# Side work queued behind the newest split of weights on ScalarE and VectorE, and a first exponential on constants, in a Griffin-style decoder layer

## The chip, the core and the metric

One core of a Trainium2 chip runs the whole kernel. The metric is device time in microseconds, the median of the timed runs. Times inside the kernel come from one profiled execution; "at 73.25" is 73.25 us after that span's start. The engines are TensorE (PE; its weight loads are PEld), VectorE (DVE), ScalarE (ACT), GpSimd (POOL) and SyncE (SP, which here only issues DMAs). PSUM is the memory in which PE accumulates; SBUF is the working memory of all engines.

## What is computed

The reference is one decoder layer on 256 tokens of width 2048, in float32. Cut to what matters here:

```python
h = rmsnorm(x, norm_mix_g)
u = h @ w_in                                   # 2048 x 12288
c, b, xa, za, q, f, iv, og, ga, gb = split(u)  # 8 fields of 1024, 2 of 2048
ya = b * causal_dwconv3(c * xa, conv_w) * silu(za)
log_f = log(lb + (1 - lb) * sigmoid(f)); kk = (1 - lb) * sigmoid(-f)
o  = hgrn2_chunked(silu(q), kk, iv, log_f)     # gated linear recurrence, 8 heads of 128
yb = rmsnorm_per_head(o) * hg_norm_g * silu(og)
m  = sigmoid(ga) * (ya @ w_a_out) + sigmoid(gb) * (yb @ w_b_out)
x  = x + m @ w_o
x  = x + sigmoid(rmsnorm(x, ple_norm_g) @ w_ple_gate) * (p @ w_ple_proj)
return rmsnorm(x, final_norm_g)
```

## The kernel before

**Products in three parts.** A float32 product is made from two rounded halves of each factor: hi*hi + hi*lo + lo*hi. `split(pos)` makes the halves of a piece of weights of 256 x 512: ACT rounds `raw` to `whi` (L118), DVE subtracts to get `wlo` (L119). `put` does the same for activations (L152, L153, tiles `xh` and `xl`, and the like). `product` issues the three matmuls (L825, L826, L827), 128 x 128 by 128 x 512 each.

**Steps.** The list `steps` runs over all weights in pieces; a step has 12 matmuls (2 blocks of 128 rows of weights, 2 tiles of 128 tokens, 3 parts) and adds to the two PSUM banks of its group. A group is 512 columns of one product. In order: 16 groups of 8 steps for f, q, iv, og, c, xa, za, b, each field in two halves (f is steps 0 to 7, q 8 to 15, iv 16 to 23, og 24 to 31 and so on, to step 127); four rounds of ga, gb, A and B (8, 8, 4 and 4 steps, to step 223); four groups O (224 to 255); then PP (1 step) and PG (8 steps) four times: PP0 is 256, PG0 257 to 264, PG2 275 to 282, PP3 283 and the last PG 284 to 291. The last PG is written out by itself at the end, in three passes over its eight steps: all 512 columns for the first token tile in one bank, and two times 256 columns for the second.

**What comes ahead of PE.** `load` brings raw weights in pairs of steps, 1024 KB, in three buffers, on SP's DMA queue. `whi` and `wlo` have four buffers each, so split p of that pool can't start before step p-4 has ended; from step 286 on they come from a pool `late` with six buffers. Before the matmuls of step `pos`, the program makes splits up to `pos + ahead(pos)`; `ahead` is 3, and from step 277 on it grows by one a step to 8.

**Side work.** What follows a group's sums is written as generators, the epilogues `ep_f`, `ep_q` and so on: each copies its sums out of PSUM, computes, turns the result through DRAM (`turned`: four DMAs out, one back, then a transpose on DVE) and makes operands for later products. `advance()` lets every live epilogue go on to its next `yield` at the end of each step. Some that matter below: `ep_iv` copies the sums of iv into `v` (L202); `ep_f` takes logarithms (L264 to L268); `hgrn` starts with `y` (L377), makes exponentials and tiles `X` for products on PE (L324, L433, and L444 to L446, which read the tile `a` written at L328); `ep_pg` empties a PG group's two banks with a sigmoid on ACT (L615), and `ep_pp` a PP group's (L605). PSUM has four banks with the tag "g", two for each group, so a group takes the banks of the group two before it.

**Who sets the order.** The program text is not the order of the queues. A scheduler orders each engine's instructions when the kernel is compiled: it takes what it reckons to be ready, so side work may stand ahead of a split that comes earlier in the text, or far ahead of its own place. Buffers are handed out in the same pass. When the kernel runs, each engine takes its own queue in that fixed order. `tc.keep_in_program_order(ins)` puts one instruction behind everything traced before it on its engine. `tc.issue_after(ins)` is a block: what is traced in it on the engine of `ins` is queued behind `ins`; it adds no semaphore and touches no other engine.

## Time and profile before

| | |
|---|---|
| timed runs, median (lowest to highest of 3) | 838.65 us (838.03 to 839.04) |
| the profiled execution | 840.08 us |
| its span, first to last instruction | 838.3 us |
| mean granted PE clock | 0.994 |
| PE, PEld, DVE, ACT, POOL busy, us | 823.8, 683.5, 531.7, 432.7, 84.1 |
| DMA, mean over the span | 218 GB/s |

The profile gives, for groups of instructions, the line, the engine, the tiles written and read, the shapes and the count; then the busy time and the mean of one, and the idle time of the engine just before, with what ended it. A name such as whi stands for all buffers of that tile. In a timeline, each row has the start, the time taken and, in brackets, the idle time before it with its releaser. Matmuls overlap, and each row shows 0.39 us for one that follows the one before it after 0.23; a few matmuls are missing from the record, and rows of equal kind are merged (x2). The granted clock is the share of PE's full clock that was let through.

### The profile page before, as it was taken

What the parts mean: (1) busy time and instruction counts of PE and PEld (TensorE: products, weight loads), DVE (VectorE), ACT (ScalarE), POOL (GpSimd) and SP (SyncE); (2) the same over time, 40 slices, a digit from 0 to 9 for tenths busy, and PEclk for the clock granted to TensorE, in tenths of its full rate; (3) what the DMA queues carried; (4) which work ended last, traced back from release to release, by engine and by line L of the source; (5) the groups of instructions that cost most, each with busy time, mean ns of one, the idle gap of its engine ahead of it and who ended that gap; (6) DMA issues with size and microseconds to landing.
All of it is one profiled execution on the core that took longest, in us unless ns stands there. A gap on an engine that the chain in (4) does not pass through costs nothing.

```text
span 838.3 us, 9794 instructions
## 1 busy us (share of the span) xinstructions
PE 823.8 (98%) x3752; PEld 683.5 (82%) x3752; DVE 531.7 (63%) x600; ACT 432.7 (52%) x562; POOL 84.1 (10%) x76
## 2 busy tenths in 40 slices
PE   8998999999999999999999999999999999999995
PEld 5886888888888888888888888888888888888885
DVE  6557596794776686785655555545545665566672
ACT  7565564445564663545543543543443555565553
POOL 1001062001000152100001001001001000002110
PEclk9999999999999999999999999999999999999998
DMA  9975555646866555657657655655754878775442
GB/s 334 370 252 203 187 192 180 221 156 228 283 206 239 194 179 184 211 181 230 229 194 232 219 197 189 229 195 187 258 200 164 296 281 301 251 244 209 174 151 101
DMA packets 39792, 183.01 MB, mean 218 GB/s; under 512 B 4544, under 2 KB 13760, under 8 KB 21824
## 3 DMA queue, kind: packets, MB, share of 16 engines
q1 hardware_dynamic: 39312, 181.81, 62.6%
q8 instruction: 29, 0.48, 0.2%
q10 hardware_dynamic: 432, 0.56, 0.2%
q14 instruction: 19, 0.16, 0.1%
HBM read 170.82 MB, written 11.53 MB: 218 GB/s over the span
## 4 chain that ended last, share of the span: by engine, by line
PE 88%; issue 1%; ACT 0%; DVE 0%; POOLq 0%; POOL 0%
PE g L826 29%; PE g L827 29%; PE g L825 29%; PE s L324 1%; PE s L433 0%; PE s L445 0%; PE s L446 0%; PE s L444 0%; ACT xs L656 0%; DVE wlo L119 0%; ACT t L639 0%; DVE t L635 0%; POOLq L989 0%; POOL r L651 0%; ACT t L634 0%
## 5 line engine op out<-in xcount | busy, mean ns | idle before, releaser
L119 DVE TENSOR_TENSOR wlo<-raw,whi 128x1024 fp32r<-128x1024 f32 (+1 forms) x294 | 367.4, 1256 | 256.5 <-ACT whi L118 255.5
L118 ACT ACTIVATE whi<-raw 128x1024 fp32r<-128x1024 f32 (+1 forms) x294 | 308.0, 1053 | 338.1 <-PE g L827 313.0
L825 PE MATMUL g<-whi,xh 128*128 128x512 f32 (+1 forms) x912 | 353.2, 388 | 3.3 <-ACT whi L118 3.3
L826 PE MATMUL g<-wlo,xh 128*128 128x512 f32 (+1 forms) x912 | 352.7, 387 | 0.8 <-DVE wlo L119 0.8
L827 PE MATMUL g<-whi,xl 128*128 128x512 f32 (+1 forms) x912 | 351.9, 386 | 0.0
L825 PEld LDWEIGHTS g<-whi,xh 128*128 128x128 f32 x912 | 171.6, 188 | 38.9 <-ACT whi L118 5.1
L826 PEld LDWEIGHTS g<-wlo,xh 128*128 128x128 f32 x912 | 171.8, 188 | 36.1 <-DVE wlo L119 2.3
L827 PEld LDWEIGHTS g<-whi,xl 128*128 128x128 f32 x912 | 171.7, 188 | 34.3
L826 PE MATMUL g<-wlo,mh 128*128 128x512 f32 x128 | 49.6, 389 | 0.0
L825 PE MATMUL g<-whi,mh 128*128 128x512 f32 x128 | 49.5, 389 | 0.0
L827 PE MATMUL g<-whi,ml 128*128 128x512 f32 x128 | 49.5, 389 | 0.0
L569 POOL TENSOR_TENSOR t<-ga,gb 128x512 f32<-128x512 f32 x8 | 14.1, 1788 | 254.1 <-DVE gb L565 254.1
L827 PEld LDWEIGHTS g<-whi,ml 128*128 128x128 f32 x128 | 24.0, 188 | 5.0
L825 PEld LDWEIGHTS g<-whi,mh 128*128 128x128 f32 x128 | 24.0, 188 | 5.0
L826 PEld LDWEIGHTS g<-wlo,mh 128*128 128x128 f32 x128 | 24.0, 188 | 4.9
L825 PE MATMUL g<-whi,yaTh 128*128 128x512 f32 x64 | 24.9, 389 | 0.0
L826 PE MATMUL g<-wlo,yaTh 128*128 128x512 f32 x64 | 24.9, 389 | 0.0
L827 PE MATMUL g<-whi,yaTl 128*128 128x512 f32 x64 | 24.9, 389 | 0.0
L825 PE MATMUL g<-whi,ybTh 128*128 128x512 f32 x64 | 24.9, 389 | 0.0
L826 PE MATMUL g<-wlo,ybTh 128*128 128x512 f32 x64 | 24.9, 389 | 0.0
L827 PE MATMUL g<-whi,ybTl 128*128 128x512 f32 x64 | 24.9, 389 | 0.0
L352 POOL TENSOR_TENSOR X<-t,kT 128x256 f32<-128x256 f32 x12 | 11.1, 922 | 107.0 <-ACT t L366 71.7
(147 smaller groups left out, 542.1 us busy)
## 6 DMA issues: line engine op xcount, KB each, us to landing
raw<-in_w_in SPq DMA_DIRECT2D x91, 1024.0 KB, 4.8
raw<-in_w_o SPq DMA_DIRECT2D x16, 1024.0 KB, 5.8
raw<-in_w_pg SPq DMA_DIRECT2D x16, 1024.0 KB, 4.8
turn<-t SPq DMA_DIRECT2D x72, 128.0 KB, 2.7
t<-turn SPq DMA_DIRECT2D x18, 512.0 KB, 5.0
raw<-in_w_a SPq DMA_DIRECT2D x8, 1024.0 KB, 5.0
raw<-in_w_b SPq DMA_DIRECT2D x8, 1024.0 KB, 5.0
raw<-in_w_in SPq DMA_DIRECT2D x9, 512.0 KB, 7.7
```

What stands on the lines that cost most here:

```text
L118: nc.scalar.activation(out=hi[:, s], in_=src[:, s], func=AF.Copy)
L119: nc.vector.tensor_tensor(out=lo[:, s], in0=src[:, s], in1=hi[:, s].bitcast(F32), op=ALU.subtract)
L324: nc.tensor.matmul(bk[:, s], X[:, 0, h, :], X[:, 1, h, :], start=True, stop=True)
L352: eng.tensor_tensor(out=xv[:, w, :, :, half, :], in0=ev[:, :, blk, :, half, :], in1=src[:, :, blk, :, half, :], op=ALU.mult,)
L569: nc.gpsimd.tensor_tensor(out=spread(m, t), in0=blocks(ga[:, s]), in1=blocks(gb[:, s]), op=ALU.add)
L825: nc.tensor.matmul(psum, oh, hi, start=first, stop=False)
L826: nc.tensor.matmul(psum, oh, lo, start=False, stop=False)
L827: nc.tensor.matmul(psum, ol, hi, start=False, stop=last)
```

## The change

- `split` keeps its two newest instructions, one on ACT and one on DVE, in `state["splits"]`.
- A new function `step(e)` lets an epilogue run to its next `yield` inside `issue_after` of both. All calls of `next` on epilogues now go through it, those of `advance` and the first one of each epilogue. So what an epilogue puts on ACT or DVE is queued behind the newest split that the program had traced by then. In the steady part that is the split three steps ahead, later up to eight. POOL, PE and SP are not tied, and neither are `put_x`, `begin`, `add_squares`, `norm_of_x`, `last_half` and the last `last_norm`, which are not called through an epilogue.
- After the memset of the constant `mhalf`, an exponential of it is written to a new small tile `table`, the first ACTIVATE of the program.
- The pad at the head of the pool `small` grows from 8 to 64 columns, with its memset.

```diff
-PAD_CONST, PAD_SMALL = 8, 8
+PAD_CONST, PAD_SMALL = 8, 64
...
-        nc.scalar.activation(out=hi[:, s], in_=src[:, s], func=AF.Copy)
-        nc.vector.tensor_tensor(
+        a = nc.scalar.activation(out=hi[:, s], in_=src[:, s], func=AF.Copy)
+        v = nc.vector.tensor_tensor(
             out=lo[:, s], in0=src[:, s], in1=hi[:, s].bitcast(F32), op=ALU.subtract
         )
+        state["splits"] = (a.ins, v.ins)
...
     nc.gpsimd.memset(mhalf, -0.5)
+
+    nc.scalar.activation(out=sc(8, "table", 1), in_=mhalf, func=AF.Exp)
...
-    def advance():
-        for e in list(active):
+    def step(e):
+
+        a, v = state["splits"]
+        with tc.issue_after(a), tc.issue_after(v):
             try:
                 next(e)
             except StopIteration:
                 active.remove(e)
+
+    def advance():
+        for e in list(active):
+            step(e)
...
             active.append(ep_f(0, waiting))
-            next(active[-1])
+            step(active[-1])
...
             active.append(epilogues[kind](j, psum))
-            try:
-                next(active[-1])
-            except StopIteration:
-                active.pop()
+            step(active[-1])
```

## The prediction

> Steps are TensorE's, numbered 0 to 291 as in the section on the kernel; "split p" makes the high and low weights of step p.

> **What bounds the kernel now.** I read the page first: engine shares, clock, chain.

> ```profile
> PE 823.8 (98%) x3752; PEld 683.5 (82%) x3752; DVE 531.7 (63%) x600; ACT 432.7 (52%) x562; POOL 84.1 (10%) x76
> ...
> PEclk9999999999999999999999999999999999999998
> ...
> PE 88%; issue 1%; ACT 0%; DVE 0%; POOLq 0%; POOL 0%
> ```

> TensorE (PE) is busy for 98% of the span, and the chain that ended last is matmuls. VectorE (DVE) and ScalarE (ACT) matter only where they make PE wait. So the second view is the list of PE's waits (total us, times, longest):

> ```profile
> PE g L825 <- ACT whi L118: 3.3, 3, 1.7
> PE s L718 <- DVE warm L714: 1.5, 1, 1.5
> PE g L826 <- DVE wlo L119: 0.8, 2, 0.5
> ```

> That is little. Two of the waits for whi (1.35 and 0.26) and one of those for wlo lie in the first 11 us; the 1.72 and 0.53 left are one place, at 75 us. Third view, ACT's timeline there:

> ```profile
> 62.70 1.99 ACT L118 ACTIVATE whi<-raw 128x1024 fp32r<-128x1024 f32 x2
> ...
> 67.05 0.20 ACT L268 ACTIVATE lfl<-t 128x8 f32<-128x8 f32 x1
> 72.77 1.37 ACT L202 ACTIVATE v<-g,r1r 128x512 f32<-128x512 f32 x2 [5.52 <-PE g L827]
> 74.03 3.89 ACT L118 ACTIVATE whi<-raw 128x1024 fp32r<-128x1024 f32 x4
> ```

> ACT sits idle for 5.52 us until PE has finished step 23, because v, which reads that step's sums, stands ahead of splits 24 to 27. Split 24 is what PE needs next. Its weights were issued at 56.86 and landed 7.6 us later, at 64.4; those of 26 and 27 landed at 69.3. So order alone made PE wait. Fourth view, stretches there (busy us of PE, PEld, DVE, ACT, POOL, then the granted clock):

> ```profile
> 70.60:74.00 3.40, 2.81 (x13) 1.99 (x11) 2.21 (x2) 1.23 (x2) 1.17 (x2) 1.00 0.08 31
> 74.00:77.40 3.40, 1.74 (x6) 1.16 (x7) 2.29 (x2) 3.40 (x5) 0.00 (x0) 1.00 0.00 0
> 77.40:80.80 3.40, 3.40 (x9) 2.64 (x8) 3.40 (x4) 1.12 (x2) 0.00 (x0) 0.51 0.36 82
> ```

> After a stretch in which PE was idle for 49% (1.66 of 3.40), the clock is granted at half for 3.4 us.

> **The gain at 75 us.** A split of step p takes the buffer of step p-4, so where its row waits for PE it starts as step p-4 ends. Split 21 starts at 57.13, split 30 at 86.09: 28.96 us for nine steps. A plain step takes 2.72 (796.11 to 798.83 at the end, the same at 91.53 to 94.25), so nine take 24.48. The place costs 4.48: some 2.7 of hole and 1.8 of half clock.

> With the change v, traced in step 23 (by then split 26 has been traced), is queued behind split 26. Splits 24, 25 and 26 need the ends of steps 20, 21, 22 (65.3, 68.0, 70.7, in steps of 2.72 from 57.1) and their weights (64.4, 64.4, 69.3): whi of 24 is there by 66.4, wlo by 67.6, and PE wants them at 73.25. The logarithms of L264 to L268 (traced in step 22, 2.7 us with their table load) now stand behind split 25, from 69 to 72; split 26 has until 78.7. What is late next? Nothing within 5 us. I take the whole **-4.48**. If the half clock does not come in every run, it is 2.7: the ends are -2.7 and -4.5.

> **What the ties delay.** They are orders, not semaphores, and no instruction is added. Side work of step p may not start before split p+3, which starts as step p-1 ends; that is before the sums of step p exist, so copies out of PSUM (PE's accumulators) lose nothing while the weights are there in time. What had run far ahead loses most: y (L377) ran at 70.75 and is first read at 104.78. Traced in step 32, it now follows wlo of split 35 (101.59 to 102.81) and ends by 104.9 at its 2.10 us; the products that need it start at 110.53, behind some 3 us of exponentials and multiplications, so I count nothing. The tightest place: the two masked copies into a (L328, 0.74 each), at 181.20 now, ahead of wlo 62. Behind it (whi 181.27 to 182.34, wlo to 183.6) they end at 185.1, and PE reads a at 186.51. It stands 1.4 us clear; without that cover each microsecond late would cost one. SP's and GpSimd's orders are not tied, but transposes' DMAs wait for tied work, and the weights behind them on SP's queue with them; splits keep about two steps of lead, so again nothing. Price: 0, bounds -0.3 (wlo at 733.6 is a hair late now) and +1.5.

> **The loss at the end.** From step 276 on, the lead over PE grows from 3 to 8 steps, so the tie reaches further: the work of step 282 (the last of group PG2) is queued behind **split 290**. ACT now:

> ```profile
> 798.83 1.06 ACT L118 ACTIVATE whi<-raw 128x1024 fp32r<-128x1024 f32 x1 [1.66 <-PE g L827]
> 800.45 2.96 ACT L118 ACTIVATE whi<-raw 128x1024 fp32r<-128x1024 f32 x3 [0.55 <-DMA raw<-in_w_pg]
> 803.59 0.69 ACT L615 ACTIVATE t<-g,r2r 128x512 f32<-128x512 f32 x1 [0.18 <-PE g L827]
> 804.18 2.00 ACT L118 ACTIVATE whi<-raw 128x1024 fp32r<-128x1024 f32 x2
> 806.08 0.68 ACT L615 ACTIVATE t<-g,r2r 128x512 f32<-128x512 f32 x1
> ...
> 809.18 1.04 ACT L118 ACTIVATE whi<-raw 128x1024 fp32r<-128x1024 f32 x1
> ```

> The rows hold splits 284, 285 to 287, 288 and 289, and 290. The first L615 empties PG2's first PSUM bank at 803.59 to 804.28. Four banks "g" exist; PG2 holds two, PP3 (step 283) two, so the final pass, from 806.79, must take the one that L615 frees. Behind split 290 that comes later, since split 290 waits for the last load of weights:

> ```profile
> L105 SPq DMA_DIRECT2D raw<-in_w_pg x1: 327/327/327, 803.9 to 803.9; - x1
> ...
> DMA to landing us min/median/max: 4.8/4.8/4.8
> ```

> It is issued at 803.93, when wlo of an earlier pair frees a buffer, and lands at 808.73. whi of 290: 808.76 to 809.81. L615: to about 810.40. PE goes on at 810.43 instead of 806.79: **+3.64**. The load hangs on PE's pace (its buffer goes back through two loads to the end of step 278), so being 4.48 earlier does not shorten this hole. PE is idle for over a stretch of 3.4; however the stretches fall, one of them is 53% idle or more, above the 49% that halved the clock at 77.4. I add half of 3.41: **+1.7**. Bounds: 2.5 (an earlier load) and 7 (two halved stretches). VectorE's tied half (L618) feeds no bank.

> [...]

> **The table and the pads.** The first table load starts when the first x lands:

> ```profile
> 4.02 1.28 ACT L152 ACT_TABLE_LOAD   x1 [4.02 <-DMA t<-in_xT]
> ...
> 9.27 1.15 ACT L118 ACTIVATE whi<-raw 128x512 fp32r<-128x512 f32 x2 [1.20 <-DMA raw<-in_w_in]
> ```

> The load and a short exponential (0.21, L754) move into ACT's idle first 4 us, after mhalf (0.92). Split 0 then starts when its weights land (4.62) instead of 5.73, and PE starts about 1.1 earlier. But step 1 waits for weights that land at 9.24, whatever ACT does: PE only reaches that wait sooner. Price 0; bounds -0.4 and, through the clock, +1.7 (third rival). The larger pad memset costs GpSimd between 0.10 (8 columns) and 0.95 (1024), in time that ACT idles. The pads' 56 columns and the new tile's 8 move all tiles allocated behind them by 256 bytes. No row shows a price for an address; steps over different operand tiles all take 2.72, and a hundredth off would be under 3 us over all: taken as 0.

> **Sum.** -4.48 + 3.64 + 1.7 + 0 = +0.9. The profiled execution took 840.08 (span 838.3 and 1.8 around it), so it would take 841.0. The median of the timed runs, 838.65, lies 1.4 lower; I put the same difference on it: **839.5**.

> **Rivals.**
> 1. The hole at the end does not open: the load of 290 comes early, or the final pass finds a bank. For it: weight loads take from 3.4 us (762.33 to 765.78, a small one) to 8.6 (741.38 to 749.98) in this trace. Against it: 3.6 us would have to vanish. 838.65 - 4.48 = 834.2.
> 2. The hole opens, but the clock stays whole: -4.48 + 3.64, so 837.8. [...] Against it stands 49% at 74.0 to 77.4.
> 3. The other side: step 0 ends near 8.4 instead of 9.5, so PE idles about 1.5 us before 9.95 and again 0.5 before 10.68. If both fall into one stretch it is 59% idle and the clock halves: +1.7, 841.2. Against: now 0.9 us idle there (27%) do not do it. It decides between 27% and 49%, hence on how the stretches fall.
> 4. The change does not do what it says: another wait keeps the place at 75 us, and the end is paid: 838.65 + 5.34 = 844.0. Against: the weights' landings above.

> **Chances.** Forecast 0.49 (its own range 837.5 to 841.5); rivals 0.19, 0.07, 0.15, 0.10. I count 0.2% (1.7 us) as about what a measurement of this kernel can tell from no change. Faster: rival 1 and 0.04 of the forecast, 0.23. Slower: rivals 3 and 4 and 0.13 of the forecast, 0.38. Same: the rest, 0.39. The range goes from rival 1 to just above rival 3, 834.0 to 842.3; rival 4 and the tails are left out.

> **What would show it.** Right: in PE's waits the 1.7 at 75 us is gone and the clock whole there; split 24 before v; near 802 to 806 a wait of PE's L825 of about 3.6 for L615, which stands behind split 290 and its DMA, and a halved stretch behind it; the first whi near 4.7, the second step's still at 9.3. Wrong: PE goes from step 283 to 284 without a wait (rival 1), or a new wait of an L324, L433 or L444 product for X, kT or a (the ties delay more than I allow).

## The result and the profile after

| | before | after |
|---|---|---|
| timed runs, median of 6 (lowest to highest), us | 838.93 (838.03 to 839.83) | 843.82 (842.37 to 844.76) |
| ratio, with its 95% interval | 1 | 1.0057 (1.0044 to 1.0070) |
| the profiled execution, us | 840.08 | 842.37 |
| its span, us | 838.3 | 840.6 |
| its mean granted clock | 0.994 | 0.995 |

The change costs 4.9 us. In the changed kernel `product` stands in L834, L835 and L836 (before: L825 to L827), the sigmoid of PG in L618 (L615), the copy of PP's sums in L608 (L605), `v` in L205 (L202), the transpose in L197 (L194); `split` keeps L118 and L119. The page's busy times and its chain:

```profile
PE 824.0 (98%) x3752; PEld 683.3 (81%) x3752; DVE 528.3 (63%) x600; ACT 435.4 (52%) x563; POOL 91.5 (11%) x76
...
PE 94%; DMA 2%; issue 1%; ACT 1%; DVE 1%; SPq 0%; POOLq 0%; POOL 0%
```

PE does the same work. New in the chain are 2% of DMA and 1% each of ACT and DVE: weights that were waited for. PE's waits (total us, times, longest) show where:

```profile
PE g L834 <- ACT t L618: 3.4, 1, 3.4
PE g L834 <- ACT xh L155: 1.5, 1, 1.5
...
PE g L834 <- ACT whi L118: 1.2, 2, 0.8
```

The 1.7 at 75 us is gone; there are two waits that the kernel before did not have. I take the places in order of time.

**At 75 us**, ACT's timeline after:

```profile
71.00 1.04 ACT L118 ACTIVATE whi<-raw 128x1024 fp32r<-128x1024 f32 x1
72.23 1.37 ACT L205 ACTIVATE v<-g,r1r 128x512 f32<-128x512 f32 x2 [0.19 <-PE g L836]
73.50 1.05 ACT L118 ACTIVATE whi<-raw 128x1024 fp32r<-128x1024 f32 x1
```

v stands behind the splits up to 26, ACT idles 0.19 us ahead of it instead of 5.52, and PE does not stop.

**At 747 us** is the wait that I had not forecast. DVE after:

```profile
743.04 1.23 DVE L119 TENSOR_TENSOR wlo<-raw,whi 128x1024 fp32r<-128x1024 f32 x1 [1.49 <-ACT whi L118]
745.76 1.23 DVE L119 TENSOR_TENSOR wlo<-raw,whi 128x1024 fp32r<-128x1024 f32 x1 [1.49 <-ACT whi L118]
746.91 1.24 DVE L197 STREAM_TRANSPOSE t<-t 128x1024 f32<-128x1024 f32 x1
```

The transpose turns the last group of O, which ended with step 255 at 725.4; from it L155 makes the operands `xh` of steps 263 and 264. The two rows of `wlo` are splits 265 and 266. In the kernel before, the transpose follows split 263:

```profile
745.72 1.23 DVE L119 TENSOR_TENSOR wlo<-raw,whi 128x1024 fp32r<-128x1024 f32 x1 [4.36 <-ACT whi L118]
746.86 1.24 DVE L194 STREAM_TRANSPOSE t<-t 128x1024 f32<-128x1024 f32 x1
```

In the changed kernel its data is read back by this DMA, which took 5.5 us, so it was there at 742.16:

```profile
736.65 0.33 SPq L193 DMA_DIRECT2D t<-turn  x1
```

The transpose starts 4.75 us later, behind the low weights of split 266, though DVE was idle for 1.49 us just ahead of that split. PE has by then done the 12 matmuls of step 265 (PP1, the tile `ph`), which the scheduler put ahead of step 263, and its next matmul comes 1.94 us after the last instead of 0.23: a hole of 1.71.

**At the end**, ACT after:

```profile
797.43 4.85 ACT L118 ACTIVATE whi<-raw 128x1024 fp32r<-128x1024 f32 x5 [0.53 <-DMA raw<-in_w_pg]
805.71 1.06 ACT L118 ACTIVATE whi<-raw 128x1024 fp32r<-128x1024 f32 x1 [3.43 <-DMA raw<-in_w_pg]
806.68 1.25 ACT L618 ACTIVATE t<-g,r2r 128x512 f32<-128x512 f32 x2
807.81 1.05 ACT L118 ACTIVATE whi<-raw 128x1024 fp32r<-128x1024 f32 x1
808.76 1.08 ACT L608 ACTIVATE pw<-g 128x512 f32<-128x512 f32 x2
```

L618 stands behind split 290, whose weights were issued at 800.91 and landed at 805.69; ACT idles 3.43 us in front of it. L608, which empties PP3's banks, stands even behind split 291. PE's next matmul starts at 807.40, 3.83 after the last one at 803.57: a hole of 3.60. The stretches of both holes and the one behind the second (busy us of PE, PEld, DVE, ACT, POOL, then the granted clock, the DMA share and GB/s):

```profile
746.17:749.58 3.41, 1.86 (x9) 1.23 (x8) 3.07 (x3) 2.19 (x5) 0.00 (x0) 1.00 0.62 255
804.20:807.60 3.40, 0.20 (x1) 0.20 (x2) 0.89 (x2) 1.89 (x3) 0.00 (x0) 1.00 0.21 87
807.61:811.02 3.41, 3.41 (x9) 2.66 (x9) 3.41 (x6) 3.38 (x8) 0.35 (x1) 0.50 0.01 2
```

The second hole is followed by 3.41 us at half clock, the first one, in this execution, is not. The profiled executions close: 840.08 - 4.48 (the place at 75 us) + 1.71 + 3.60 + 1.71 (an estimate, half of 3.41) = 842.62, and 842.37 was taken. In the medians the same change is 4.9 and not 2.3, which the experiments have to explain.

**At the start**, the table load and the exponential do move:

```profile
1.17 1.28 ACT L135 ACT_TABLE_LOAD   x1 [1.17 <-PEq L989]
...
8.86 1.15 ACT L118 ACTIVATE whi<-raw 128x512 fp32r<-128x512 f32 x2 [1.18 <-DMA raw<-in_w_in]
```

PE's first product starts at 5.84 instead of 6.40, and step 1 waits for its weights as before: PE 0.38 us for `whi` (0.26 before), ACT 1.18 for the load ahead of it (1.20 before).

### The profile page after: what moved, and what is told of

It is laid out like the page before. It is cut to its first block, busy times and chain, and to the rows that moved or that the text cites. A ratio compares the mean times of both kernels' runs of the same rounds, so it can differ in the third digit from the quotient of the medians.

```text
span 840.6 us, 9805 instructions
## 1 busy us (share of the span) xinstructions
PE 824.0 (98%) x3752; PEld 683.3 (81%) x3752; DVE 528.3 (63%) x600; ACT 435.4 (52%) x563; POOL 91.5 (11%) x76
## 4 chain that ended last, share of the span: by engine, by line
PE 94%; DMA 2%; issue 1%; ACT 1%; DVE 1%; SPq 0%; POOLq 0%; POOL 0%
PE g L836 31%; PE g L835 31%; PE g L834 31%; PE s L327 1%; DMA raw<-in_w_pg 1%; DMA raw<-in_w_in 1%; ACT whi L118 1%; DVE wlo L119 1%; PE s L436 0%; PE s L449 0%; PE s L448 0%; PE s L447 0%; ACT xs L659 0%; ACT t L642 0%; SPq L713 0%
## 5 line engine op out<-in xcount | busy, mean ns | idle before, releaser
L119 DVE TENSOR_TENSOR wlo<-raw,whi 128x1024 fp32r<-128x1024 f32 (+1 forms) x294 | 360.2, 1229 | 272.4 <-ACT whi L118 271.7
L118 ACT ACTIVATE whi<-raw 128x1024 fp32r<-128x1024 f32 (+1 forms) x294 | 308.9, 1053 | 353.2 <-PE g L836 314.2
L834 PE MATMUL g<-whi,xh 128*128 128x512 f32 (+1 forms) x912 | 352.9, 388 | 6.2 <-ACT t L618 3.4
L835 PE MATMUL g<-wlo,xh 128*128 128x512 f32 (+1 forms) x912 | 352.6, 387 | 0.0
L836 PE MATMUL g<-whi,xl 128*128 128x512 f32 (+1 forms) x912 | 352.0, 386 | 0.0
L834 PEld LDWEIGHTS g<-whi,xh 128*128 128x128 f32 x912 | 171.6, 188 | 42.0 <-ACT t L618 3.9
L835 PEld LDWEIGHTS g<-wlo,xh 128*128 128x128 f32 x912 | 171.7, 188 | 34.9 <-DVE wlo L119 1.2
L836 PEld LDWEIGHTS g<-whi,xl 128*128 128x128 f32 x912 | 171.7, 188 | 34.9 <-DVE xl L156 0.5
L835 PE MATMUL g<-wlo,mh 128*128 128x512 f32 x128 | 49.6, 389 | 0.0
L834 PE MATMUL g<-whi,mh 128*128 128x512 f32 x128 | 49.5, 389 | 0.0
L836 PE MATMUL g<-whi,ml 128*128 128x512 f32 x128 | 49.5, 389 | 0.0
L836 PEld LDWEIGHTS g<-whi,ml 128*128 128x128 f32 x128 | 24.0, 188 | 5.0
L834 PEld LDWEIGHTS g<-whi,mh 128*128 128x128 f32 x128 | 24.0, 188 | 5.0
L835 PEld LDWEIGHTS g<-wlo,mh 128*128 128x128 f32 x128 | 24.0, 188 | 4.9
L373 POOL TENSOR_TENSOR t<-b 128x512 f32<-128x512 f32 x10 | 20.8, 2085 | 65.3 <-DMA raw<-in_w_in 33.6
L355 POOL TENSOR_TENSOR X<-t,kT 128x256 f32<-128x256 f32 x12 | 14.1, 1173 | 99.4 <-ACT t L369 57.7
L834 PE MATMUL g<-whi,yaTh 128*128 128x512 f32 x64 | 24.9, 389 | 0.0
L835 PE MATMUL g<-wlo,yaTh 128*128 128x512 f32 x64 | 24.9, 389 | 0.0
L836 PE MATMUL g<-whi,yaTl 128*128 128x512 f32 x64 | 24.9, 389 | 0.0
L834 PE MATMUL g<-whi,ybTh 128*128 128x512 f32 x64 | 24.9, 389 | 0.0
L835 PE MATMUL g<-wlo,ybTh 128*128 128x512 f32 x64 | 24.9, 389 | 0.0
```

The source lines that it names most:

```text
L118: a = nc.scalar.activation(out=hi[:, s], in_=src[:, s], func=AF.Copy)
L119: v = nc.vector.tensor_tensor(out=lo[:, s], in0=src[:, s], in1=hi[:, s].bitcast(F32), op=ALU.subtract)
L355: eng.tensor_tensor(out=xv[:, w, :, :, half, :], in0=ev[:, :, blk, :, half, :], in1=src[:, :, blk, :, half, :], op=ALU.mult,)
L373: nc.gpsimd.tensor_tensor(out=er, in0=br, in1=ref, op=ALU.subtract)
L834: nc.tensor.matmul(psum, oh, hi, start=first, stop=False)
L835: nc.tensor.matmul(psum, oh, lo, start=False, stop=False)
```

## The experiments

All twelve kernels compute the whole reference. Each was timed on one chip against runs of the kernel before, whose median was 839.03 to 839.11. Ratios are to it, with 95% intervals.

### The parts: table without ties, ties without table

e1_table is the kernel before with only

```diff
-PAD_CONST, PAD_SMALL = 8, 8
+PAD_CONST, PAD_SMALL = 8, 64
+    nc.scalar.activation(out=sc(8, "table", 1), in_=mhalf, func=AF.Exp)
```

> The kernel before with the exponential on constants and the larger pad alone, no ties. Theory A (the ties make the whole loss; the table load is hidden by the loads of step 1): within 1 us of before, 0 to -0.9, PE's first matmul about 0.6 to 1.1 us earlier and the second step 0.4 earlier at most. Theory B (the earlier start empties PE ahead of step 1 and halves the clock there in most runs): +0.8 to +1.7 over before, a halved stretch within the first 15 us. Theory C (the 256 bytes by which all later tiles move cost something everywhere): a difference spread over the span, steps no longer 2.72 us.

Measured: 838.44, ratio 0.9995 (0.9986 to 1.0003). The exponential and the moved addresses neither cost nor gain anything that is measured. In its profile the hole at 75 us is there in full (PE's longest wait for `whi` is 1.7 us, as before), but the clock stays whole behind it:

```profile
71.58:74.99 3.41, 1.91 (x9) 1.26 (x7) 1.35 (x1) 2.14 (x3) 0.27 (x1) 1.00 0.00 0
...
75.00:78.40 3.40, 2.66 (x10) 1.91 (x11) 3.21 (x3) 3.01 (x4) 0.00 (x0) 1.00 0.00 0
```

So the half clock that I counted at that place does not come in every execution.

e2_ties is the changed kernel without the exponential and with the old pad.

> The changed kernel without the exponential and with the old pad: the ties alone. Theory A: 0 to 0.9 us above the changed kernel, some 4.9 to 5.5 above before, with both new holes (step 263, final pass) in the profile. Theory B: 1 to 1.7 us below the changed kernel. Theory C: differs from the changed kernel all over the span.

Measured: 843.36, ratio 1.0047 (1.0035 to 1.0060). Both new waits of PE are there (3.5 for L617, 1.5 for xh); the ties carry the whole loss.

### Which steps' ties gain and lose

In e3_lead3 a tie always goes to split p+3, however far ahead the splits are:

```diff
-        state["splits"] = (a.ins, v.ins)
+        state["split", pos] = (a.ins, v.ins)
...
-        a, v = state["splits"]
+        a, v = state["split", min(state["pos"] + LEAD, len(steps) - 1)]
```

> The changed kernel, but side work of step p is tied to split p+3 to the end, instead of to the newest split: only the places of the sigmoids of step 282 and of what follows move on ScalarE and VectorE. If the wait of the final pass is worth its hole and one halved stretch: 3.6 + 1.7 = 5.3 us below the changed kernel, so about 838.5, with the hole at step 263 still there. Rival (PE merely waits for something else there, such as the last load): no more than 2 us below the changed kernel.

Measured: 837.67, ratio 0.9987 (0.9976 to 0.9998). The hole at the end is gone (PE's list has no wait for L618), so it came from the lead that grows there; the wait of 1.5 us for xh stays. Here that hole is followed by a half clock:

```profile
747.98:751.39 3.41, 1.82 (x7) 0.97 (x6) 3.08 (x5) 2.65 (x5) 0.00 (x0) 1.00 0.38 159
...
751.39:754.80 3.41, 3.41 (x9) 2.68 (x9) 0.84 (x3) 0.10 (x1) 0.00 (x0) 0.50 0.88 305
```

e4_until224 is the changed kernel with ties only in the steps up to 223 (here and below, `step` enters `issue_after` only under a condition on the step):

```diff
-        with tc.issue_after(a), tc.issue_after(v):
+        with ExitStack() as ties:
+            if state["pos"] < 224:
+                ties.enter_context(tc.issue_after(a))
+                ties.enter_context(tc.issue_after(v))
```

> The changed kernel with ties only up to step 223, so the groups O, PP and PG are free as before. If the gain at step 24 is real and the rest of the loss comes from the two late holes: no hole from step 24 to the end, 838.9 - 4.5 = 834.4 (down to 833.5 with the start's share). If the loss comes from ties in the earlier part or from the start: above 836.

Measured: 836.61, ratio 0.9966 (0.9955 to 0.9978). PE's waits hold no hole any more behind the start: 1.5 us for `warm` and 0.9 for the first `whi`, both in the first 6 us. The gain is 2.5 us and not the 4.5 that I had expected.

e5_step23 is the kernel before with the table and the pad, and a tie in step 23 alone (`state["pos"] == 23`); of all queues, only the place of v changes by this tie.

> The exponential on constants, the larger pad, and ties at step 23 alone (so that v stands behind split 26). If the whole gain is v's place: as fast as the kernel tied to step 223, 836.6 (some 2.5 below before), no hole at 75 us and none later. Rival (the other ties up to 223 gain too, or v's place is only a part): 1 us or more slower than 836.6.

Measured: 836.64, ratio 0.9971 (0.9960 to 0.9981). The same 2.5 us: v's place is the whole gain, and the ties of the other steps up to 223 neither gain nor cost anything that is measured.

### The hole at 747 us

e8_no255 is the changed kernel without the ties of step 255 (`!= 255`).

> The changed kernel without the ties of step 255 alone. If that tie makes the hole at step 263: the hole is gone, 1.7 us and a part of a halved stretch less than the changed kernel, 841.0 to 842.0; the wait of the final pass stays. Rival: the hole stays and so does the time, 843.8.

Measured: 841.81, ratio 1.0028 (1.0017 to 1.0038): 2.0 us less than with them (843.82). The wait for xh is gone. Step 255 ends at 725.6 in it, 0.2 later than in the changed kernel, but the DMA that reads the data back is issued at 734.97 and the transpose starts 7 us earlier:

```profile
738.76 1.23 DVE L119 TENSOR_TENSOR wlo<-raw,whi 128x1024 fp32r<-128x1024 f32 x1 [1.82 <-ACT whi L118]
739.90 1.24 DVE L197 STREAM_TRANSPOSE t<-t 128x1024 f32<-128x1024 f32 x1
```

e7_step255 is the kernel before with a tie in step 255 alone.

> The kernel before with ties at step 255 alone, where ep_o takes the sums of O3; no exponential, old pad. If the hole at step 263 comes from this one tie (the sums' additions behind split 258 move the DMA that brings the turned x back behind a load of weights, and its transpose behind split 266): a hole of 1.5 to 1.9 us before step 263's first matmul, waiting for xh; in part of the runs a halved stretch; 1.5 to 3.5 us over before. Rival (the hole comes of PE being earlier, or of the ties of steps 256 to 263): as before, no hole there.

Measured: 840.39, ratio 1.0019 (1.0009 to 1.0028): 1.3 us lost, a little less than expected. The one hole of 1.5 to 1.9 did not come: PE has two gaps there, of 0.2 and 0.4, and slower starts behind them, some 0.9 together. So this tie alone moves the queues and costs time, but the full hole is seen only together with the other ties. The queues of the two compiled kernels say how. The transpose stands on DVE behind split 266 and no longer behind split 263; on SP, the load of PP's weights and one more load of PG's now stand ahead of the DMA that reads the data back:

```profile
738.14 1.77 SPq L190 DMA_DIRECT2D turn<-t  x4
740.02 0.40 SPq L103 DMA_DIRECT2D raw<-in_w_pp  x1
741.48 0.35 SPq L105 DMA_DIRECT2D raw<-in_w_pg  x1
742.37 0.33 SPq L192 DMA_DIRECT2D t<-turn  x1
```

In the kernel before:

```profile
735.47 1.78 SPq L188 DMA_DIRECT2D turn<-t  x4
737.36 0.39 SPq L105 DMA_DIRECT2D raw<-in_w_pg  x1
740.05 0.34 SPq L190 DMA_DIRECT2D t<-turn  x1
740.48 0.38 SPq L103 DMA_DIRECT2D raw<-in_w_pp  x1
```

No tie is laid on SP or PE, and yet their orders change. The scheduler, given a later place for the tied additions and copies of step 255, chose other places for DMAs, the transpose, and PE's own matmuls (that it does so because it reckons all that hangs on them later is my reading of it, and no run shows it): in the kernel before, the matmuls of PP1 are spread between those of steps 263 and 264, here they stand in one block ahead of them. The data landed at 749.88 in e7 and the transpose started at 752.22, so of its lateness the last 2.3 us (4.75 in the changed kernel) are DVE's queue.

### The hole at the end

e6_step282 is the kernel before with a tie in step 282 alone.

> The kernel before with ties at step 282 alone, no exponential, old pad. If the final pass can only take a bank of PG2, which L618 (L615 of before) empties behind split 290: a hole of 3.5 us at the start of the final pass and a halved stretch in most runs, 4.5 to 5.5 us over before. Rival (the pass takes a bank of PP3, which is free earlier): a hole under 1.5 us, at most 2 us over before.

Measured: 839.36, ratio 1.0005 (0.9995 to 1.0015). L617 (the sigmoid) does stand behind split 290 and its late load, and PE hardly waits: its list has no wait for L617, and of the stretch 807.95 to 811.36 it is idle for 0.01 us. ACT there:

```profile
807.56 1.28 ACT L607 ACTIVATE pw<-g 128x512 f32<-128x512 f32 x2 [0.87 <-PE g L838]
810.14 1.06 ACT L118 ACTIVATE whi<-raw 128x1024 fp32r<-128x1024 f32 x1 [1.30 <-DMA raw<-in_w_pg]
811.11 1.25 ACT L617 ACTIVATE t<-g,r2r 128x512 f32<-128x512 f32 x2
```

The copy of PP3's sums comes at 807.56, its first half ends at 808.16, and PE's first matmul of the final pass starts at 808.21: the pass takes the bank that this copy frees. My sentence that the final pass must take PG2's bank was wrong.

e9_282_283 is the kernel before with the ties of steps 282 and 283.

> The kernel before with ties at steps 282 and 283 alone, no exponential, old pad. With step 282 alone the final pass took a bank of PP3, which the copies into pw (L607 there) emptied at once. If the hole needs both, with pw now behind split 291: a hole of about 3.5 us ahead of the final pass and a halved stretch in most runs, 4.5 to 5.5 us over before. Rival (the hole of the changed kernel has another cause): at most 1 us over before.

Measured: 844.75, ratio 1.0072 (1.0059 to 1.0085): +5.7. PE's next matmul comes 3.89 after the last (808.05 to 811.94), a hole of 3.66, and half clock behind it (its wait in PE's list, then the stretch):

```profile
PE g L836 <- ACT t L617: 3.5, 1, 3.5
```

```profile
811.58:814.99 3.41, 3.05 (x7) 2.47 (x8) 3.41 (x6) 3.39 (x7) 0.00 (x0) 0.50 0.01 2
```

e10_no283 is the changed kernel without the tie of step 283.

> The changed kernel without the ties of step 283 alone: on ScalarE only the two copies into pw move, from behind split 291 to ahead of split 290. If one free pair of banks is enough: the hole of the final pass falls from 3.6 us to about 0.3, and the time by 4.5 to 5.5 us, to 838.5 to 839.3, with the hole at step 263 still there. Rival: no change from the changed kernel, 843.8.

Measured: 837.91, ratio 0.9994 (0.9985 to 1.0003): 5.9 less than the changed kernel. The copy of PP3's sums is back ahead of split 290 and of L618:

```profile
803.62 1.28 ACT L608 ACTIVATE pw<-g 128x512 f32<-128x512 f32 x2 [0.88 <-PE g L839]
806.33 1.06 ACT L118 ACTIVATE whi<-raw 128x1024 fp32r<-128x1024 f32 x1 [1.43 <-DMA raw<-in_w_pg]
807.29 1.24 ACT L618 ACTIVATE t<-g,r2r 128x512 f32<-128x512 f32 x2
```

So the tie of step 282, which puts L618 behind split 290, makes no hole without that of step 283, which puts the copy of PP3's sums behind split 291; together they make it. The tie of step 283 alone was not run. The profile before speaks for its being harmless too: there L615 has emptied a bank by 804.28, and PP3's sums are copied only at 806.65, without a wait of PE.

### A longer start

e11_warm is e4 with `WARM = 12` instead of 8, and e12_before_warm the kernel before with it (the matmuls on zeros that run ahead of the first product, L718 in the kernel before).

> The kernel tied up to step 223, with 12 instead of 8 matmuls on zeros ahead of the first step. In several profiles the clock is still granted at half when the first step runs, until 9.6 to 12.9 us; with PE busy to 6.5 us instead of 5.05 the full clock should come by 7 us in every run. If that start costs time in most runs: 0.5 to 1.5 us below the kernel tied up to step 223 (836.6). Rival (the first steps wait for their weights anyway): no difference, or up to 0.5 us more for the later start.

> The kernel before with 12 instead of 8 matmuls on zeros. If the late full clock at the start costs time in most runs: 0.5 to 1.5 us below before, with the hole at step 24 unchanged. Rival: no difference.

Measured: e11 835.87, ratio 0.9961 (0.9949 to 0.9974), the best of all; e12 839.78, ratio 1.0001 (0.9993 to 1.0010). The intervals of e11 and e4 overlap, and that of e12 includes no change, so four more warm matmuls are not shown to be worth anything; the gain of e11 is that of the ties up to step 223. Seven of e12's eleven runs have a mean clock of 0.994 or 0.995, against six of the 21 runs of the kernel before beside them, so more of them may hold a half clock at 75 us, which could hide a small gain at the start. That stays open.

## Why the prediction was wrong

Taken by its own steps, the terms are, in us (each measured one is a difference of medians, good to about 1):

| step | predicted | measured by runs |
|---|---|---|
| gain at 75 us | -4.48 | -2.5 (e4, e5) |
| what the ties delay | 0, at most +1.5 | +2.0 (changed kernel less e8); +1.3 alone (e7) |
| end: hole and half clock | +3.64 + 1.7 = +5.3 | +5.9 (changed kernel less e10); +5.7 alone (e9) |
| table and pads | 0 | -0.6 (e1), its interval includes 0 |
| sum | +0.9 | -2.5 + 2.0 + 5.9 = +5.4; the whole change +4.9 |

**"I take the whole -4.48" failed in size.** The order was as forecast, to the split, and the hole of 2.7 went. The 1.8 of half clock belongs to the profiled execution and to a minority of the runs. In the fourteen profiles, a mean granted clock of 0.996 to 0.998 goes with no stretch at half clock between the first rise and PE's last matmul, 0.994 or 0.995 with one, and 0.992 with two. Of 31 runs of the kernel before, timed beside e5 to e8, 11 had a mean of 0.993 to 0.995, as the profiled one (0.994), and 20 one of 0.996 to 0.998. The runs of e5 all have 0.996 or 0.997, and against those 20 (median 839.02) they gain 2.4, near the hole's 2.7. The 11 have a median of 840.04, only 1.0 higher and not 1.7, so more than this one stretch differs between the groups; the start can (last section).

I named 2.7 as the other end and chose the wrong one. The profiled execution had lain 1.4 us over the median, and that was a sign: the half clock was in it and not in most runs, and I carried the 1.4 over to a kernel from which I had just taken that half clock.

**"Price: 0" failed.** I had followed the tied instructions, and the DMAs behind them, and allowed two steps of lead. I took the rest of every queue as fixed. It is not: the tie of step 255 alone made the scheduler queue loads ahead of the read-back and the transpose behind three more splits. The price, 2.0, lies outside my bound of 1.5: the hole alone is 1.71, and in most runs it seems to bring half clock as well. Of six runs of the changed kernel four have a clock of 0.992 to 0.993 and two 0.995, the profiled one among these. One more stretch of 3.41 us at half clock lowers the mean by 0.002 (1.7 of 840). That is how the medians come to differ by more than the two profiled executions: the one before had a half clock that most runs have not, and the one after lacked one that most runs have.

**The end was right in place, price and releaser** (3.60 for 3.64, and half clock behind it), by a reason of which half was missing. That L615 goes behind split 290 does not suffice (e6). My working never asked where L605 would go, whose step is also tied; where it stays, a gap of 0.17 is left there (e10's profile). The right number was in part luck: it came from one of two conditions that both had to hold. Nor is my step from "53% idle or more" to half clock safe: in e2's profile two stretches in a row, 54 and 49% idle, were followed by the whole clock (last section). After, the stretch was 94% idle.

**The table and the pads cost nothing that is measured**, as forecast (e1; e2 against the changed kernel), and PE's earlier start gave nothing that is measured: step 1 still waits for its weights (0.38 us of PE's time, against 0.26 before).

**The rivals.** 1 (no hole at the end) did not come, and its 834.2 would not have either: e4, which has neither new hole, takes 836.6, for the gain is 2.5. 2 (whole clock behind the hole at the end) did not hold in the profiles of after, e8 and e9; it did in that of e2, which still took 843.23, so its 837.8 was out of reach even there. 3 (a halved stretch at the start) did not come: e1 loses nothing, and no profile has a fall of the clock in its first 70 us. 4's time, 844.0, is near what came, for a reason that did not: the place at 75 us was not kept. I had named a new wait for an operand as proof against me. One did come, but for `xh`, in `product`, and not in the products of `hgrn` where I had looked for it.

## What to carry to other kernels

An order that is imposed on one engine is an input to the scheduler: compare the whole queues of both kernels, SP's and PE's too, before calling the untied ones unchanged. Tie only the instruction that is out of place (here v in step 23, worth the whole 2.5 us), since a tie to "the newest" means a different distance wherever the lead grows, and ask of each buffer that comes free behind a tie whether another one serves instead. A half clock behind a hole is worth as much as its share of runs: read it from the granted clocks of several runs, not from the one that was profiled.

## What the runs showed of the clock

```profile
804.77:808.19 3.42, 1.57 (x7) 0.95 (x6) 2.05 (x2) 0.05 (x2) 0.00 (x0) 1.00 0.68 273
808.19:811.60 3.41, 1.74 (x8) 1.44 (x9) 2.33 (x3) 3.41 (x5) 0.00 (x0) 1.00 0.00 0
```

They are busy for 46 and 51%, and the clock stayed whole. What is counted within a stretch stays open.

The start varies too. Until the first rise, matmuls follow each other after 0.43 us instead of 0.23, as they do in the stretch at half clock at 77.45 to 80.86 of the kernel before. In e2, e6 and e9 the rise came only at 12.6 to 12.9 us, and `v` starts at 74.23 to 74.63 us, against 72.12 to 73.18 in the other eleven profiles; PE is busy without a break up to 74.08 in e6 and to 74.30 in e9, where in the kernel before the hole has begun at 73.41. So e6's profiled execution took 841.62, 1.54 over that of the kernel before, with the same hole and half clock at 75 us and no hole at the end. The mean granted clock does not show this, since the record begins with the first rise (4.0 to 5.0 us of the profile after, ahead of its rise at 5.48, counts as 1.00). How often the start is late in the other runs is not on record.
